# A token-by-weight scaling kernel: six tile sizes replaced by eight equal tiles of 16 tokens

## The chip, the core and the metric

The kernel runs on one core of one Trainium2 chip. Four parts of the core matter here: VectorE (DVE) and ScalarE (ACT), which multiply; SyncE (SP), which computes nothing and issues transfers; and 16 DMA engines, which move data between the chip's main memory (HBM) and the on-chip memory (SBUF, 128 partitions). SP and ACT each own one queue of transfers, and both queues run on the same 16 DMA engines. The metric is the device time of one execution in microseconds (us), as the median of several runs.

## The reference

Every token is a vector of 512 floats, and it is written out twice, each time multiplied by one of its two expert weights. The expert indices are not used.

```python
batch, seq, hidden, k = 16, 1024, 512, 2
def reference(x, expert_indices, expert_weights):
    x_expanded = x[:, :, np.newaxis, :].repeat(k, axis=2)
    return (x_expanded * expert_weights[..., np.newaxis]).astype(np.float32)
```

That is 16,384 tokens: 33.6 MB of x are read, 67.1 MB are written, and the weights are 0.13 MB.

## The kernel before

The 16,384 tokens are 128 for each of the 128 partitions. They are cut into groups of T tokens per partition, and inside a group partition p holds T tokens that follow one another in memory, so that what one partition loads or stores is one contiguous run. I call such a run a row: a load of n tokens has rows of n x 2 KB, a store of n tokens rows of n x 4 KB, and each transfer has 128 rows, 8 for each DMA engine. The groups are five of 24 tokens and one of 8 (`groups`).

Three pools hold the data in SBUF. `w_pool` has all weights in one tile. `x_pool` has two buffers of 24 tokens (TX), `o_pool` two buffers of 12 tokens of output (TO). Together they take 193 KB of each partition.

Three transfers on SP's queue bring the weights at the start. `load(i)` brings input tile i on ACT's queue; the first tile comes in six pieces of 4 tokens, so that computing can begin early, and all others in one transfer. Two loads are issued ahead, and load i + 2 is called after tile i has been computed, since it needs that tile's buffer.

For each token there are two multiplies of a 128x512 slice by one weight per partition. Two of every three go to VectorE, the third to ScalarE (`c % 3 == 2`). When 12 tokens are done, or the tile is at its end, SP stores them. An output buffer can be written again only when the store that reads it, two stores earlier, has landed; an input buffer can be loaded again only when both engines have read all of it.

The framework that builds the kernel adds the semaphore waits, and may move an instruction a few places on its engine's own queue. Each queue is worked in order: a transfer that stands behind a waiting multiply on ACT is not issued before that multiply has started.

Of the kernel before, what the change touches and what calls it, by code (L numbers as in the profile page):

```python
# [1 line left out]

# [4 lines left out]


@with_exitstack
def kernel(  # L10
    ctx: ExitStack,
    tc: tile.TileContext,
    x: bass.AP,
    expert_indices: bass.AP,
    expert_weights: bass.AP,
    out: bass.AP,
):
    nc = tc.nc

    batch, seq, hidden = x.shape  # L20
    k = expert_weights.shape[-1]
    P = nc.NUM_PARTITIONS
    ntok = batch * seq
    assert ntok % P == 0
    A_TOTAL = ntok // P

    f32 = mybir.dt.float32
    row = k * hidden
    TX = 24
    TO = 12  # L30

    groups = [[24], [24], [24], [24], [24], [8]]
    assert sum(sum(g) for g in groups) == A_TOTAL

    xf = x.rearrange("b s h -> (b s) h")
    of = out.rearrange("b s k h -> (b s) (k h)")
    wf = expert_weights.rearrange("b s k -> (b s) k")

    w_pool = ctx.enter_context(tc.tile_pool(name="w_pool", bufs=1))
    x_pool = ctx.enter_context(tc.tile_pool(name="x_pool", bufs=2))  # L40
    o_pool = ctx.enter_context(tc.tile_pool(name="o_pool", bufs=2))

    w_tile = w_pool.tile([P, A_TOTAL * k], f32)

    def rows(of_all, done, T):
        return of_all[done * P : (done + T) * P, :].rearrange(
            "(p a) n -> p (a n)", a=T
        )

    T0 = sum(groups[0])  # L50
    G = len([g for g in groups[1:] if sum(g) == T0])
    head = (1 + G) * T0
    nc.sync.dma_start(out=w_tile[:, : T0 * k], in_=rows(wf, 0, T0))
    nc.sync.dma_start(
        out=w_tile[:, T0 * k : head * k].rearrange("p (g n) -> p g n", g=G),
        in_=wf[T0 * P : head * P, :].rearrange("(g p a) n -> p g (a n)", g=G, p=P),
    )
    nc.sync.dma_start(
        out=w_tile[:, head * k :], in_=rows(wf, head, A_TOTAL - head)
    )  # L60

    tiles = []
    done = 0
    for group in groups:
        T = sum(group)
        a0 = 0
        for n in group:
            tiles.append((done, T, a0, n))
            a0 += n
        done += T  # L70

    loaded = []

    def load(i):
        if i >= len(tiles):
            return
        done, T, a0, n = tiles[i]
        x_tile = x_pool.tile([P, TX * hidden], f32)
        src = rows(xf, done, T)
        step = TX // 6 if i == 0 else n  # L80
        for at in range(0, n, step):
            nc.scalar.dma_start(
                out=x_tile[:, at * hidden : (at + step) * hidden],
                in_=src[:, (a0 + at) * hidden : (a0 + at + step) * hidden],
            )
        loaded.append(x_tile)

    for i in range(2):
        load(i)
    for i, (done, T, a0, n) in enumerate(tiles):  # L90
        x_tile = loaded[i]
        outr = rows(of, done, T)
        for t in range(n):
            if t % TO == 0:
                o_tile = o_pool.tile([P, TO * row], f32)
            for kk in range(k):
                c = (done + a0 + t) * k + kk
                o = t % TO * row + kk * hidden
                if c % 3 == 2:
                    nc.scalar.mul(  # L100
                        out=o_tile[:, o : o + hidden],
                        in_=x_tile[:, t * hidden : (t + 1) * hidden],
                        mul=w_tile[:, c : c + 1],
                    )
                    continue
                nc.vector.tensor_scalar(  # L106
                    out=o_tile[:, o : o + hidden],
                    in0=x_tile[:, t * hidden : (t + 1) * hidden],
                    scalar1=w_tile[:, c : c + 1],
                    scalar2=None,  # L110
                    op0=mybir.AluOpType.mult,
                )
            if (t + 1) % TO == 0 or t + 1 == n:
                at = t // TO * TO
                nc.sync.dma_start(  # L115
                    out=outr[:, (a0 + at) * row : (a0 + t + 1) * row],
                    in_=o_tile[:, : (t + 1 - at) * row],
                )
        load(i + 2)

# [1 line left out]
_INS = ['x', 'expert_indices', 'expert_weights']  # L122
_OUTS = [((16, 1024, 2, 512), 'float32')]


# [23 lines left out]
```

## Time and profile before

| What | Value |
|---|---|
| median of three runs | 240.58 us (239.81 to 240.78) |
| span of the profiled execution, first to last instruction | 238.9 us, 1.7 us less than the median |
| bytes moved | 100.81 MB, mean 422 GB/s |
| VectorE busy | 69.0 us, 171 multiplies |
| ScalarE busy | 54.9 us, 85 multiplies and one table load |
| stores | 10 of 6,144 KB and 1 of 4,096 KB |
| loads | 6 of 1,024 KB, 4 of 6,144 KB, 1 of 2,048 KB |
| weights | 24 KB, 96 KB and 8 KB |

The page of the profile gives busy time per engine, and then the span in 40 slices of 6 us, where a digit is the busy share of a slice in tenths. The share of DMA is the mean over the 16 DMA engines. q1 is SP's queue and q10 is ACT's. A DMA queue's line tells packets, megabytes, and the time its packets took as a share of 16 engines' time; asked for a window, the same line is counted over the packets that start in the window. Besides its rows, each transfer has up to 16 packets of 4 bytes, which signal that an engine has finished. A line of a window of time gives start and end, length, busy time and number of instructions of VectorE, ScalarE and GpSimd, the TensorE clock (of no use here), the DMA share, and GB/s. A packet is counted where it starts, so that short windows can show shares over 1.

### The profile page before, as it was taken

To read this page: it belongs to the slowest core of one execution; us is meant where nothing else is said; L and a number is where in the kernel's file an instruction comes from. 1 tells how busy PE (TensorE), PEld (TensorE's weight loads), DVE (VectorE), ACT (ScalarE), POOL (GpSimd) and SP (SyncE) were. 2 spreads that over 40 slices of the span, in tenths; PEclk is the share of its full clock that TensorE was granted. 3 is DMA by queue.
4 is the path that set the end of the run, shared out by engine and by line. 5 is a ranking of instruction groups with operands and counts; after the bars stand their busy time and mean duration, and the time that the engine had idled before them with its cause. 6 is when DMAs were issued, how large, how long until landed. Compare 5 with 4: busy or idle time off the path is not lost.

```text
span 238.9 us, 364 instructions
## 1 busy us (share of the span) xinstructions
DVE 69.0 (29%) x171; ACT 54.9 (23%) x86; POOL 0.2 (0%) x4
## 2 busy tenths in 40 slices
DVE  0890300004609100190063037003706406415000
ACT  0870300004308000170071034003406106213000
POOL 0000000000000000000000000000000000000000
DMA  6999999999999999999999999999989899999994
GB/s 244 420 443 395 495 395 395 494 428 395 428 494 395 413 494 411 395 446 469 403 411 502 395 420 453 436 411 428 469 379 496 381 428 469 436 411 428 436 439 197
DMA packets 3986, 100.81 MB, mean 422 GB/s; under 512 B 1168, under 2 KB 1168, under 8 KB 1168
## 3 DMA queue, kind: packets, MB, share of 16 engines
q1 hardware_dynamic: 2400, 67.24, 65.2%
q10 hardware_dynamic: 1584, 33.56, 33.1%
q14 instruction: 2, 0.02, 0.0%
HBM read 33.69 MB, written 67.11 MB: 422 GB/s over the span
## 4 chain that ended last, share of the span: by engine, by line
DMA 66%; DVE 13%; another core or an unknown queue 11%; issue 0%; DVEq 0%; SPq 0%
DMA out_dram<-o_tile 54%; DVE o_tile L106 13%; DMA x_tile<-in_x_dram 11%; DVEq L144 0%; DVEq L106 0%; SPq L115 0%
## 5 line engine op out<-in xcount | busy, mean ns | idle before, releaser
L106 DVE TENSOR_SCALAR o_tile<-x_tile,w_tile 128x512 f32<-128x512 f32 x171 | 69.0, 480 | 149.3 <-DMA out_dram<-o_tile 105.3
L100 ACT ACTIVATE o_tile<-x_tile,w_tile 128x512 f32<-128x512 f32 x85 | 53.6, 709 | 155.5 <-DMA out_dram<-o_tile 116.8
L100 ACT ACT_TABLE_LOAD x1 | 1.3, 1283 | 6.7 <-DMA x_tile<-in_x_dram 6.7
L133 POOL MEMSET const-bfloat16-1.0<- 128x1 bf16 x1 | 0.1, 101 | 0.0
L133 POOL MEMSET const-uint8-127<- 128x1 uint8 x1 | 0.1, 101 | 0.0
L133 POOL MEMSET const-float32-0.0<- 128x1 f32 x1 | 0.1, 98 | 0.2 <-issue 0.2
L133 POOL MEMSET const-float32-1.0<- 128x1 f32 x1 | 0.1, 98 | 0.0
## 6 DMA issues: line engine op xcount, KB each, us to landing
out_dram<-o_tile SPq DMA_DIRECT2D x10, 6144.0 KB, 33.6
x_tile<-in_x_dram ACTq DMA_DIRECT2D x4, 6144.0 KB, 43.9
x_tile<-in_x_dram ACTq DMA_DIRECT2D x6, 1024.0 KB, 10.6
out_dram<-o_tile SPq DMA_DIRECT2D x1, 4096.0 KB, 19.5
x_tile<-in_x_dram ACTq DMA_DIRECT2D x1, 2048.0 KB, 24.0
w_tile<-in_expert_weights_dram SPq DMA_DIRECT2D x1, 96.0 KB, 11.1
w_tile<-in_expert_weights_dram SPq DMA_DIRECT2D x1, 24.0 KB, 2.9
w_tile<-in_expert_weights_dram SPq DMA_DIRECT2D x1, 8.0 KB, 13.2
```

The costliest lines, as they stand in the source:

```text
L100: nc.scalar.mul(out=o_tile[:, o : o + hidden], in_=x_tile[:, t * hidden : (t + 1) * hidden], mul=w_tile[:, c : c + 1],)
L106: nc.vector.tensor_scalar(out=o_tile[:, o : o + hidden], in0=x_tile[:, t * hidden : (t + 1) * hidden], scalar1=w_tile[:, c : c + 1], scala ...
L133: nc = _bacc.Bacc("TRN2", target_bir_lowering=False, num_devices=1)
```

## The change

The groups become four of 32 tokens, each in two tiles of 16 (`groups = [[16, 16]] * 4`). Input tiles and output tiles are both 16 tokens: load rows of 32 KB, store rows of 64 KB, two buffers of each. A partition's run in memory is now 64 KB of x and 128 KB of the output for each group, and a tile takes half of it. There are 8 stores instead of 11. The first tile comes in four pieces of 4 tokens and the other seven in one load each, 11 loads as before. The weights come in two transfers on ACT's queue instead of three on SP's: those of the first group behind the first piece of the first tile, all others behind its last piece.

On ACT's queue of the built kernel, the load of the third tile stands behind the first multiply of the second tile; in the kernel before it stood ahead of it.

```diff
-    TX = 24
-    TO = 12
+    TX = 16
+    TO = 16
+    XB = 2
-    groups = [[24], [24], [24], [24], [24], [8]]
+    groups = [[16, 16]] * 4
-    x_pool = ctx.enter_context(tc.tile_pool(name="x_pool", bufs=2))
+    x_pool = ctx.enter_context(tc.tile_pool(name="x_pool", bufs=XB))
     o_pool = ctx.enter_context(tc.tile_pool(name="o_pool", bufs=2))
...
-    nc.sync.dma_start(out=w_tile[:, : T0 * k], in_=rows(wf, 0, T0))
-    nc.sync.dma_start(
-        out=w_tile[:, T0 * k : head * k].rearrange("p (g n) -> p g n", g=G),
-        in_=wf[T0 * P : head * P, :].rearrange("(g p a) n -> p g (a n)", g=G, p=P),
-    )
-    nc.sync.dma_start(
-        out=w_tile[:, head * k :], in_=rows(wf, head, A_TOTAL - head)
-    )
+    def first_weights():
+        nc.scalar.dma_start(out=w_tile[:, : T0 * k], in_=rows(wf, 0, T0))
+
+    def other_weights():
+        nc.scalar.dma_start(
+            out=w_tile[:, T0 * k : head * k].rearrange("p (g n) -> p g n", g=G),
+            in_=wf[T0 * P : head * P, :].rearrange("(g p a) n -> p g (a n)", g=G, p=P),
+        )
...
-        step = TX // 6 if i == 0 else n
+        step = TX // 4 if i == 0 else n
         for at in range(0, n, step):
             nc.scalar.dma_start(
                 out=x_tile[:, at * hidden : (at + step) * hidden],
                 in_=src[:, (a0 + at) * hidden : (a0 + at + step) * hidden],
             )
+            if i == 0 and at == 0:
+                first_weights()
+        if i == 0:
+            other_weights()
...
-    for i in range(2):
+    for i in range(XB):
         load(i)
...
-        load(i + 2)
+        load(i + XB)
```

## The prediction

> **What bounds the kernel now.** I read the page's busy slices first, then its DMA queues, then windows of time, and the chain that ended last only to see the end. Busy slices and queues on the page:
>
> ```profile
> DMA  6999999999999999999999999999989899999994
> q1 hardware_dynamic: 2400, 67.24, 65.2%
> q10 hardware_dynamic: 1584, 33.56, 33.1%
> L106 DVE TENSOR_SCALAR o_tile<-x_tile,w_tile 128x512 f32<-128x512 f32 x171 | 69.0, 480 | 149.3 <-DMA out_dram<-o_tile 105.3
> ```
>
> VectorE works 69 us of 238.9. The 16 DMA engines are busy in every slice but the first and last: 65.2% + 33.1% = 98.3% of the span, 234.8 us per engine. q1 is SP's queue (stores, and in this kernel the weights), q10 is ACT's (loads). The time is therefore what each engine has to move, plus the ends, plus any stretch in which its queues are empty. Windows (length, DVE, ACT, POOL busy, clock, DMA share, GB/s):
>
> ```profile
> 1.00:2.00 1.00, 0.00 (x0) 0.00 (x0) 0.00 (x0) 1.00 0.39 57
> 2.00:3.00 1.00, 0.00 (x0) 0.00 (x0) 0.00 (x0) 1.00 0.64 189
> 140.00:180.00 40.00, 12.85 (x32) 10.02 (x16) 0.00 (x0) 1.00 1.00 434
> 235.00:236.00 1.00, 0.00 (x0) 0.00 (x0) 0.00 (x0) 1.00 0.84 360
> 236.00:237.00 1.00, 0.00 (x0) 0.00 (x0) 0.00 (x0) 1.00 0.08 33
> ```
>
> The middle is full at 434 GB/s. First rows run from about 1.7 us; shares of rows that start fall off after 235, and the last store, issued at 218.4 and landing in 19.5, ends at 237.9.
>
> One row of a transfer (one partition's contiguous run) is one packet, so windows with one size of row price it. Stores alone, 200 to 218 us (48 KB rows) and 228.5 to 234.5 (32 KB):
>
> ```profile
> q1 hardware_dynamic: 176, 7.86, 100.9%
> ...
> q1 hardware_dynamic: 80, 2.62, 101.1%
> ```
>
> 100.9% of 16 engines x 18 us over 160 rows (the other 16 packets only signal) is 1.816 us for 48 KB; 101.1% of 96 us over 80 is 1.213 us for 32 KB. The step is 0.603 us per 16 KB, so a 64 KB row is 2.419 us by extrapolation. From 4 to 13 us (first loads and weights):
>
> ```profile
> q10 hardware_dynamic: 501, 3.64, 96.2%
> q1 hardware_dynamic: 659, 0.11, 6.5%
> ```
>
> 444 rows of 8 KB in 138.5 us: 0.311 us each; small packets 0.014 us each. How two queues share an engine, 140.5 to 159 us (both 48 KB rows) and 176 to 192 us (48 KB stores, 16 KB loads):
>
> ```profile
> q1 hardware_dynamic: 82, 3.98, 49.7%
> q10 hardware_dynamic: 81, 3.93, 49.1%
> ...
> q1 hardware_dynamic: 116, 4.92, 71.3%
> q10 hardware_dynamic: 123, 2.02, 29.4%
> ```
>
> Equal numbers of rows, whatever their size: the engine alternates row by row. The second pair prices 16 KB at 0.612 us (29.4% of 256 us over 123). Last, how late a new transfer starts on a busy engine: load 4 is issued at 127.86, and from 128 to 132.4 only this of it had begun:
>
> ```profile
> q10 hardware_dynamic: 1, 0.05, 2.6%
> ```
>
> So 4.5 to 5 us. Likewise the first store: issued at 13.38, six rows begun by 17.6. Into an idle engine it is 1 us (issue 0.73, rows at 1.7).
>
> VectorE's restarts come from its timeline (start, length, count; in brackets the wait before):
>
> ```profile
> 8.64 2.07 DVE L106 TENSOR_SCALAR o_tile<-x_tile,w_tile 128x512 f32<-128x512 f32 x5 [0.33 <-DMA x_tile<-in_x_dram]
> 11.23 2.07 DVE L106 TENSOR_SCALAR o_tile<-x_tile,w_tile 128x512 f32<-128x512 f32 x5 [0.52 <-DMA x_tile<-in_x_dram]
> 13.79 4.55 DVE L106 TENSOR_SCALAR o_tile<-x_tile,w_tile 128x512 f32<-128x512 f32 x11 [0.49 <-DMA x_tile<-in_x_dram]
> 57.24 6.42 DVE L106 TENSOR_SCALAR o_tile<-x_tile,w_tile 128x512 f32<-128x512 f32 x16 [27.10 <-DMA x_tile<-in_x_dram]
> ```
>
> They go with the pieces of the first load, 2.5 us apart; a multiply takes 0.401 us of such a run.
>
> **The change, part by part.** *Rows.* Each of 11 + 11 transfers of x and out puts 8 rows on each engine. Before: stores 80 x 1.816 + 8 x 1.213, loads 48 x 0.311 + 32 x 1.816 + 8 x 0.612, weights 48 x 0.014: 145.3 + 9.7 + 14.9 + 58.1 + 4.9 + 0.7 = 233.6 us (page: 234.8; the rest is slower first rows and signals). After: stores 64 x 2.419, loads 32 x 0.311 + 56 x 1.213, weights 32 x 0.014: 154.8 + 10.0 + 67.9 + 0.4 = 233.1. Gain 0.5 us. The bytes are the same. Price of the unseen 64 KB row: lower end 2.412 (the line's fixed part, 1.816 - 3 x 0.603 = 0.007 us, gone: 0.4 us more gained over 64 rows); upper end the poorest rate of a full window, 415 GB/s for 8 KB rows against 434, 4.6% of 154.8 = 7 us. I take 2.419, since three sizes lie on one line.
>
> A rule that speaks against the new layout: the Trainium skill, "DMA: Bandwidth & Descriptors", section Latency and other measured facts, has copies between HBM tensors lose rate at row pitches of large powers of two, 207 against 214 GB/s at 512 KiB. The new pitches are 64 KB (loads) and 128 KB (stores) where most were 48 and 96. By it, 3% of 154.8 us would give about 245 us, as an estimate. The smallest pitch there is four times ours, and this trace's last group, whose store pitch is 32 KB, shows 1.213 us a row on the common line; I follow the trace.
>
> *Weights.* SP loses three issues (0.37, 0.42, 0.50 us), ACT gains two of about 0.45 between the pieces of load 0. A 1 MB piece occupies the engines 2.5 us, so later pieces are still issued long before their turn. The weights the first multiply needs come 8 small packets behind piece 1: 0.1 us, inside VectorE's wait for that piece until 5.85. The rest (24 packets, 0.3 us) stands ahead of load 1, needed much later. Price at the start from -1 us (the 0.97 us lost between 1 and 3 us all regained) to +0.4 (one issue bare); I take 0, as the queue of 8 KB rows still has to start up.
>
> *Order at the head.* VectorE resumes on pieces 1 to 4 at 5.85, 8.64, 11.23, 13.79; with fewer small packets between, the fourth comes near 13.4. Then 6 multiplies at 0.401 us (6.42 over 16 in the timeline): store 0 is issued at 15.9 (before: 13.4, after 12 tokens). Until its rows start, about 20, the engines run load 1 from 13.5: 6 of 8 rows. Two remain and alternate with two store rows: load 1 ends at 13.5 + 8 x 1.213 + 2 x 2.419 = 28.0. No gap.
>
> *Loads behind a multiply.* On ACT's queue the third load is now placed behind the first multiply of tile 1, which waits for load 1. It goes out at 29 and starts about 34. Cover: store 0 still has 6 rows, 14.5 us; 3 of them run alone, until 35.2. Then 8 load rows with 7 store rows between: load 2 ends at 61.8, with 2 + 3 + 7 = 12 store rows done, so 4 rows of store 1 are left when tile 2 can start.
>
> *Steady state.* A load row and a store row take 1.213 + 2.419 = 3.63 us, eight pairs 29.1 us, and a tile needs exactly eight of each: the remainder of 4 rows is carried from tile to tile. A tile's 21 multiplies (8.4 us) hide under it; its output buffer is free, since the store two earlier ended long before. VectorE now waits for loads where it waited for stores. That costs nothing: engines stay full.
>
> *The end.* Load 7 ends at 61.8 + 5 x 29.1 = 207.1. Multiplies: landing 0.3, work 8.5, issue and start 1.0 (the idle-engine row): store 7's rows start at 216.9. The cover, 4 rows of store 6, ends at 207.1 + 9.7 = 216.8. So some 0.1 us is bare; before, the last store of 8 tokens was issued at 218.4 while the one ahead, of 205.9, landed 22.4 later: 9.9 us of cover. Each row of cover less costs 2.4 us; each more costs nothing and saves 0.1.
>
> **Sum.** Profiled execution: span 238.9 us; the median of the runs, 240.58, is 1.7 above it, and I carry that over. 238.9 - 0.5 (rows) + 0.1 (end) = 238.5 in the profile; timed, 240.2. I state 240.3.
>
> **Rivals.** *Cover short at the end.* The remainder is 3 rows or fewer when tile 7 starts, so the engines run dry while VectorE multiplies. It decides from one row: if load 2 starts after 35.2 instead of 34, a fourth store row passes alone, and three are left. For it: its lag is read with 48 KB rows, and a row of 64 KB holds an engine longer. Short lags do it too: with the idle engine's 1 us at both places, five pairs run at the head, one store row alone and seven in between, 13 in all. Against it: a short second lag after a long first one leaves six. 3 rows: 240.1 + 2.5 = 242.6; 2 rows: 245.
>
> *Long rows or pitches are slower.* No row speaks for it: 8, 16, 32 and 48 KB lie on one line. At the upper end above, 240.3 + 7 = 247; at a third of that, 242.7.
>
> *64 KB rows are not carried as such*, but as two of 32 KB: 64 more packets, 64 x (2 x 1.213 - 2.419) = 0.4 us, and loads get half the engine instead of a third, so that stores gate and the end is covered: 240.5.
>
> *Faster.* The 0.97 us of the ramp and part of the slowest engine's lag at the end go (234.8 us of work from 1.7 us would end at 236.5, the last landing is at 237.9): -0.5 - 1 gives 239.1. For it: no second queue at the start. Against it: neither lag is tied to weights in any row.
>
> **How the numbers follow.** Forecast 0.49; cover short 0.20; slow rows 0.07; split rows 0.09; faster 0.15. The limit of what can be told from no change is 0.5%, 1.2 us: below 239.4 and above 241.8. Faster 0.17 (rival, and a little of the forecast's spread), slower 0.29 (both slow rivals, and 0.02 of the forecast), same 0.54. The range runs from 239.0, the faster rival, to 242.9, cover short by one row; two rows short and most of slow rows are left out.
>
> **What the profile of the changed kernel would show.** Right: q1 with 1,024 rows of 64 KB and a share near 64.8%; stores-only windows at 2.42 us a row; twice as many bytes from q1 as from q10 in a mixed window, with equal rows; VectorE's wait mostly on x_tile, about 20 us a tile; DMA share 1.00 from 207 to 217. Wrong: a share well below 1 in that stretch (cover short), 2,048 store packets (split), a full-share window clearly under 434 GB/s (slow rows).

## The result, and the profile after

The changed kernel takes 252.14 us (median of four runs, 248.88 to 254.03) against 240.67 for the kernel before on the same chip. The ratio is 1.040, with a 95% interval of 1.037 to 1.043: 4% slower. The forecast was 240.3 and its range ended at 242.9. Medians and ranges are of all executions; the ratios, here and below, leave out those that took over 1.5% more than the fastest of their kernel (here 252.86 and 254.03). Several kernels of this study vary by up to 13 us between executions, and where a profile is of one away from the median, its time is given. The profile of the changed kernel is of an execution of 252.86 us with a span of 251.1.

From its page: busy slices of 6.3 us, DMA queues, and VectorE's largest group.

```profile
DMA  6999989999989999989989999999999998934994
q1 hardware_dynamic: 1152, 67.11, 62.7%
q10 hardware_dynamic: 2128, 33.69, 33.5%
L112 DVE TENSOR_SCALAR o_tile<-x_tile,w_tile 128x512 f32<-128x512 f32 x171 | 68.7, 481 | 160.6 <-DMA x_tile<-in_x_dram 129.2
```

The shares give the first half of the answer. They are 62.7% + 33.5% = 96.2% of 251.1 us, or 241.6 us per engine. Before it was 234.8. So the same bytes cost 6.8 us more of engine time, a mean over 16 engines. The span grew by 12.2 us, so the other 5.4 lie where the engines have nothing to do: 9.5 us now, 4.1 before. The busy slices show where: the digits 3 and 4 in slices 36 and 37, about 220 to 232 us. Windows of the changed kernel (length, DVE, ACT, POOL busy, clock, DMA share, GB/s):

```profile
60.00:100.00 40.00, 12.65 (x32) 11.27 (x19) 0.00 (x0) 1.00 1.01 420
100.00:140.00 40.00, 12.96 (x33) 8.67 (x14) 0.00 (x0) 1.00 0.99 410
140.00:180.00 40.00, 8.40 (x21) 6.85 (x11) 0.00 (x0) 1.00 0.99 407
210.00:220.00 10.00, 0.00 (x0) 0.00 (x0) 0.00 (x0) 1.00 1.00 433
220.00:230.00 10.00, 8.41 (x21) 6.85 (x11) 0.00 (x0) 1.00 0.26 111
```

Two losses, and they are different. From 60 to 180 us the engines are full, yet move 407 to 420 GB/s, where the kernel before moved 433 to 434: rows take longer in the mean. From 220 to 230 us the share is 0.26, so 7.4 us of a mean engine are empty, exactly while VectorE multiplies the last tile.

Rows priced again, first stores alone (231 to 246 us), then the long mixed stretch (20 to 200 us):

```profile
q1 hardware_dynamic: 96, 6.29, 97.0%
```

```profile
q1 hardware_dynamic: 850, 50.20, 65.8%
q10 hardware_dynamic: 860, 25.04, 34.3%
```

Alone, a 64 KB row takes 97.0% of 240 us / 96 = 2.425 us, as forecast (2.419). In the mixed stretch the megabytes make 766 rows of 64 KB and 764 of 32 KB: equal numbers, as forecast. But they take 65.8% of 2,880 us / 766 = 2.474 and 34.3% / 764 = 1.293 us. A pair costs 3.77 us, not 3.63.

These are means, and most rows do not share in the loss. Counted one by one in the trace from 20 to 200 us, 1,245 of the 1,530 rows take what was forecast, 2.42 and 1.21 us within 2%. The other 285 take longer, up to 3.28 and 2.99 us, and cost 6.3 us per engine. In the kernel before, 14 of 1,665 rows are over its prices by so much. So single rows are held up; a row of 64 or 32 KB is not slow as such.

VectorE's timeline shows what gates each tile (start, length, wait before it in brackets):

```profile
34.26 8.40 DVE L112 TENSOR_SCALAR o_tile<-x_tile,w_tile 128x512 f32<-128x512 f32 x21 [17.62 <-DMA x_tile<-in_x_dram]
...
190.37 8.80 DVE L112 TENSOR_SCALAR o_tile<-x_tile,w_tile 128x512 f32<-128x512 f32 x22 [23.24 <-DMA x_tile<-in_x_dram]
220.84 8.41 DVE L112 TENSOR_SCALAR o_tile<-x_tile,w_tile 128x512 f32<-128x512 f32 x21 [21.67 <-DMA x_tile<-in_x_dram]
```

The last tile starts at 220.84, 13.4 us later than the forecast's 207.4. But the trace has 16 completion signals for each transfer, one of each engine (it does not tell which is whose), and these tell a different story than "the load came late". The load of tile 7 completes on the first engine at 201.7, on the median engine at 207.0, and on the last at 220.65. The median engine is on the forecast's time, in part by luck, since at load 2 it was 4.5 us behind it. How far the 16 engines lie apart, as last minus first signal of one load:

```text
load                 1     2     3     4     5     6     7
kernel before     3.9 us at most
changed kernel    5.9   3.4  10.5  11.4  13.9  15.3  18.9 us
```

The queues from 202 to 220 us show the same from another side:

```profile
q1 hardware_dynamic: 116, 7.01, 89.9%
q10 hardware_dynamic: 33, 0.72, 10.0%
```

Stores take 89.9% of the engines' time here: most engines have only stores left, and a few still work on the load that everybody waits for. It lands at 220.65 us. Half of the engines have finished their part of store 6 by 223.9 (the first at 221.0), and the next store is issued only at 229.3.

### The profile page after: what moved, and what is told of

It reads as the page before. It is cut to its first block, busy times and chain, and to the rows that moved or that the text cites. A ratio compares the mean times of both kernels' runs of the same rounds, so it can differ in the third digit from the quotient of the medians.

```text
span 251.1 us, 358 instructions
## 1 busy us (share of the span) xinstructions
DVE 68.7 (27%) x171; ACT 54.6 (22%) x86; POOL 0.2 (0%) x4
## 3 DMA queue, kind: packets, MB, share of 16 engines
q1 hardware_dynamic: 1152, 67.11, 62.7%
q10 hardware_dynamic: 2128, 33.69, 33.5%
## 4 chain that ended last, share of the span: by engine, by line
DMA 50%; DVE 15%; another core or an unknown queue 14%; issue 11%; ACTq 1%; DVEq 0%; SPq 0%; ACT 0%
DMA x_tile<-in_x_dram 33%; DMA out_dram<-o_tile 16%; DVE o_tile L112 15%; ACTq L84 1%; ACTq L59 0%; ACTq L56 0%; DVEq L150 0%; DVEq L112 0%; SPq L121 0%; ACT o_tile L106 0%
```

## The experiments

The expectations name theories by letters. **G**: with load rows half as long as store rows, and row-by-row turns, a load gets one third of an engine and a tile needs exactly one third. VectorE waits for the slowest engine's load. An engine that is ahead empties its stores, then takes its loads alone, and gets further ahead; the spread grows until the end stands bare. **S**: 64 KB rows as such are slow among other traffic. **P**: the row pitches in HBM (64 and 128 KB) are slow. **W**: the place of the weights on ACT's queue does it. **R**, formed only after some of the runs: a load and a store that run in step slow each other. Spread means last minus first completion signal of a load, as above.

**Pitch: one group per tile.** With this edit a tile is contiguous in HBM: pitch 32 KB for loads, 64 KB for stores.

```diff
-    groups = [[16, 16]] * 4
+    groups = [[16]] * 8
```

> Eight groups of 16 tokens instead of four of 32: the rows stay 32 KB and 64 KB, but they follow one another without a gap in memory (pitch 32 KB and 64 KB instead of 64 KB and 128 KB). Theory P (rows of loads and stores disturb each other because the pitches are 64 KB and 128 KB): rows less slow, excess per engine clearly under the 6.5 us of the changed kernel, 243 to 249 us. Theory S (it is the size of the rows, 64 KB stores beside 32 KB loads, whatever the pitch): as the changed kernel, 249 to 254 us.

Measured: 252.04 us (three executions of 252.0 to 255.3, one of 244.44); in the profiled one, of 252.06, the load spread grows to 19.6 us. Its windows:

```profile
100.00:140.00 40.00, 12.22 (x31) 7.94 (x13) 0.00 (x0) 1.00 0.99 411
140.00:180.00 40.00, 8.40 (x21) 6.85 (x11) 0.00 (x0) 1.00 0.99 410
...
220.00:230.00 10.00, 8.30 (x21) 6.58 (x11) 0.00 (x0) 1.00 0.37 157
```

Both losses are as in the changed kernel, at half the pitch.

**Pitch: sizes that are no power of two.** Groups of 48 and 80 tokens, loads with a pitch of 96 and 160 KB, stores 192 and 320 KB (the later weights then come in one contiguous transfer).

```diff
-    groups = [[16, 16]] * 4
+    groups = [[16] * 3, [16] * 5]
```

> Groups of 48 and 80 tokens, in tiles of 16: the rows stay 32 KB and 64 KB, the pitches become 96 and 192 KB, then 160 and 320 KB, none a power of two. Theory P: rows of 1.213 and 2.418 us again, 434 GB/s where loads and stores run together, 240 to 242 us. Theory S: as the changed kernel, 249 to 254 us.

Measured: 251.17 us (three executions of 250.9 to 251.5, one of 244.20); load spreads in that of 251.53: 0.7, 3.8, 4.5, 7.3, 12.7, 19.7, 21.6 us. Windows:

```profile
20.00:60.00 40.00, 8.40 (x21) 6.85 (x11) 0.00 (x0) 1.00 1.03 445
60.00:100.00 40.00, 15.05 (x38) 13.09 (x21) 0.00 (x0) 1.00 1.00 425
100.00:140.00 40.00, 10.55 (x27) 6.85 (x11) 0.00 (x0) 1.00 0.98 407
```

P falls: at every pitch tried, three or four of four executions took 249 to 255 us, and both losses are in the traces. The two executions of 244 do not speak for P, since the next run, at the pitch of the changed kernel, has one of 245 too. The run gives something more. Here the engines start close together, and from 20 to 60 us 64 KB and 32 KB rows run at full pace (445, with 3% of starts borrowed from the next window). The pace is lost only later, while the spread grows. So neither the row sizes nor their mixture must be slow.

**Weights back on SP's queue, at the start.**

```diff
-        nc.scalar.dma_start(out=w_tile[:, : T0 * k], in_=rows(wf, 0, T0))
+        nc.sync.dma_start(out=w_tile[:, : T0 * k], in_=rows(wf, 0, T0))
...
-        nc.scalar.dma_start(
+        nc.sync.dma_start(
...
-            if i == 0 and at == 0:
-                first_weights()
-        if i == 0:
-            other_weights()
...
+    first_weights()
+    other_weights()
     for i in range(XB):
```

> The changed kernel with both weight transfers back on SP's queue at the start. Theories P and S: no effect beyond 0.5 us, 249 to 254 us. Theory W (the weights in the load queue upset the order at the head, and all that follows): 240 to 243 us.

Measured: 247.96 us (245.06 to 251.77), ratio 1.026 (1.020 to 1.033); in the profiled execution, the one of 251.77, the spread still grows to 21.8 us. Most of the loss stays without the moved weights. The ratio is below the 1.040 of the changed kernel and the intervals do not overlap, so up to a third of the loss may go with the weights; with four executions on each side, which differ by 5 to 7 us, it may also be chance.

**Stores in two halves: equal rows.** Each store of 16 tokens becomes two of 8, with 32 KB rows like the loads.

```diff
-                nc.sync.dma_start(
-                    out=outr[:, (a0 + at) * row : (a0 + t + 1) * row],
-                    in_=o_tile[:, : (t + 1 - at) * row],
-                )
+                for h in range(0, TO, 8):
+                    nc.sync.dma_start(
+                        out=outr[:, (a0 + at + h) * row : (a0 + at + h + 8) * row],
+                        in_=o_tile[:, h * row : (h + 8) * row],
+                    )
```

> The changed kernel with each store cut into two of 8 tokens, issued together: store rows of 32 KB, pitches as in the changed kernel, and loads get every second turn of an engine for equal rows. Theory P: rows still slow (5 to 7 us per engine), but the loads run ahead and the end is covered, 245 to 248 us. Theory S: rows at full pace, 240 to 242 us.

Measured: 242.71 us (242.23 to 243.13), ratio 1.009 (1.007 to 1.010). That is 9.4 of the 11.5 us, four fifths of the loss, by an edit that moves the same bytes. It changes one thing besides the row: the first half of a store can go out before the second is computed (10.27 and 15.77 us for store 0, which went out whole at 16.73). The next run has that too. Windows, then VectorE's first two waits (total, times, longest):

```profile
60.00:100.00 40.00, 16.37 (x42) 12.09 (x20) 0.00 (x0) 1.00 1.00 433
...
140.00:180.00 40.00, 8.40 (x21) 6.84 (x11) 0.00 (x0) 1.00 1.01 434
...
220.00:230.00 10.00, 0.00 (x0) 0.00 (x0) 0.00 (x0) 1.00 1.01 436
```

```profile
DVE o_tile L112 <- DMA out_dram<-o_tile: 89.1, 4, 24.2
DVE o_tile L112 <- DMA x_tile<-in_x_dram: 36.0, 4, 17.8
```

The loads now get half of an engine where they need a third, so they are early; VectorE waits mostly for stores, as it did before the change; the spread stays at 3.7 us or less; the pace is back. Both G and S allow this.

**Both halved.** The stores as just shown, and the loads halved too, the later half first. All rows of the later loads are 16 KB, those of the stores 32 KB: the ratio of the changed kernel at half its sizes.

```diff
-        step = TX // 4 if i == 0 else n
-        for at in range(0, n, step):
+        step = TX // 4 if i == 0 else n // 2
+        for at in range(0, n, step) if i == 0 else range(n - step, -1, -step):
```

> The changed kernel with every transfer cut in two: load rows 16 KB (the later half first, so that a tile still starts only when all of it has landed), store rows 32 KB. Rows are half as long, but a load still gets one third of an engine beside a store, so that tiles wait for loads, and for the slowest engine's. Theory G (the order: loads that get only their need gate every tile, engines that are ahead run out of store rows, take loads alone and get further ahead, until some are empty at the end): landings of one load spread to over 8 us between engines by the end, 243 to 252 us. Theory S (rows of 64 KB are the trouble): spread under 4 us, 240 to 242 us.

Measured: 246.22 us (245.89 to 252.35), ratio 1.021 (1.016 to 1.026). The profile is of the execution of 252.35, the others took 245.9 to 246.9. The spread is up to 11.3 us, the pace low again:

```profile
100.00:140.00 40.00, 10.16 (x26) 6.85 (x11) 0.00 (x0) 1.00 1.00 422
140.00:180.00 40.00, 8.40 (x21) 6.85 (x11) 0.00 (x0) 1.00 1.00 422
```

With 32 KB rows as the longest, and the stores of the run above, S would have full pace here; only the ratio of the rows is that of the changed kernel. S falls as the one cause. About half of the loss is here, 2.1 of 4.0%; whether longer rows add the rest is not shown.

**The kernel before, with its loads halved.** The other direction: 24 KB load rows against 48 KB store rows in the kernel that was fine.

```diff
-        step = TX // 6 if i == 0 else n
-        for at in range(0, n, step):
+        step = TX // 6 if i == 0 else n // 2
+        for at in range(0, n, step) if i == 0 else range(n - step, -1, -step):
```

> The kernel before with each load of 24 tokens cut in two (24 KB rows, later half first), its stores unchanged at 48 KB: loads get one third of an engine instead of half. Theory G: the spread between engines grows past 6 us and the kernel slows to 242 to 248 us, less than the changed kernel, since the last tile has 8 tokens. Theory S: 240.5 to 241.5 us.

Measured: 246.89 us (244.12 to 248.09), ratio 1.016 (1.009 to 1.024). In the profiled execution, of 247.95, the spread grows to 15.5 us and at one load 24.4. Windows:

```profile
140.00:180.00 40.00, 12.85 (x32) 10.02 (x16) 0.00 (x0) 1.00 1.00 413
180.00:200.00 20.00, 6.42 (x16) 5.01 (x8) 0.00 (x0) 1.00 1.00 405
```

That is 413 where the kernel before has 434. Same tiles, buffers, stores and weights; loads that get a third of the engine, and both symptoms appear. The head moved as well, though: the eight load transfers hold ACT's queue, ScalarE's table load comes only at 13.5 us, and store 0 goes out at 19.84 instead of 13.38. So the cleaner evidence for G's first half, that the ratio of row sizes starts the drift, is the two runs above, which differ by the load rows alone; this run agrees.

**Other ratios of rows.** In the next kernel a load brings 32 tokens (64 KB rows) and a store takes 8 (32 KB rows), so that loads get two thirds.

```diff
-    TX = 16
-    TO = 16
+    TX = 32
+    TO = 8
...
-    groups = [[16, 16]] * 4
+    groups = [[32]] * 4
...
-        step = TX // 4 if i == 0 else n
+        step = TX // 8 if i == 0 else n
```

> Input tiles of 32 tokens (64 KB load rows) and output tiles of 8 (32 KB store rows), two buffers each, 193 KB as in both kernels, groups and weights as in the changed kernel: a load gets two thirds of an engine, so that tiles wait for stores. Theory G: no growing spread, 240 to 242.5 us. Theory S (64 KB rows beside 32 KB rows): slow rows of 4 us per engine and more, 244 to 252 us.

Measured: 244.17 us (ten runs, 241.97 to 245.76), ratio 1.011 (1.007 to 1.015), load spreads of 2 to 4 us after the first tile (up to 11 within it). It lies between what the theories gave and settles nothing, except that 64 KB load rows can run within about 1% of the kernel before.

Then 32 KB rows on both sides, in three buffers each:

```diff
-    TO = 16
-    XB = 2
+    TO = 8
+    XB = 3
...
-    o_pool = ctx.enter_context(tc.tile_pool(name="o_pool", bufs=2))
+    o_pool = ctx.enter_context(tc.tile_pool(name="o_pool", bufs=3))
```

> Input tiles of 16 tokens in three buffers, output tiles of 8 in three buffers: load and store rows both of 32 KB, 193 KB in all, groups and weights as in the changed kernel. Theory G: a load gets half an engine, three buffers let engines differ by more before one stands empty, no growing spread, 239.5 to 241.5 us. Theory R: depends on the order in which rows meet; 240 to 246 us.

Measured: 248.49 us (244.29 to 251.19), ratio 1.018 (1.010 to 1.026). G's forecast failed. In the profiled execution, the fastest (244.29), the spread is 3 us at most for loads and 5.5 for stores, but load rows are slow in stretches, 1.27 us in the mean instead of 1.213 from 20 to 60 us:

```profile
20.00:60.00 40.00, 11.34 (x29) 9.94 (x16) 0.00 (x0) 1.00 1.00 420
```

An equal share is therefore not enough: there is a second way to lose the pace, without a large spread.

**The end alone.** The last tile of the changed kernel is cut into two of 8 tokens, so that the last store can be issued earlier.

```diff
-    groups = [[16, 16]] * 4
+    groups = [[16, 16]] * 3 + [[16, 8, 8]]
```

> The changed kernel, whose last 16 tokens are cut into two tiles of 8 (load rows 16 KB, store rows 32 KB): after the last load only 4.3 us of multiplies are left instead of 8.5, and half of the last output is queued before. Theory G: about 4 us of the 7 us in which engines stand empty at the end come back, 245 to 250 us, slow rows stay. If the end costs nothing: 249 to 254 us.

Measured: 251.26 us (250.55 to 251.66), ratio 1.041 (1.037 to 1.046): nothing gained. The empty stretch has moved ahead:

```profile
140.00:180.00 40.00, 8.40 (x21) 6.85 (x11) 0.00 (x0) 1.00 0.99 412
180.00:200.00 20.00, 8.80 (x22) 6.24 (x10) 0.00 (x0) 1.00 0.83 354
```

As it looks, once the engines have drifted, whichever tile comes late leaves the early ones without work, and a shorter last tile only changes which: the span has 8.6 us of a mean engine empty, against 9.5.

**The weights of the kernel before, on ACT's queue.** The part of the change that was priced at nothing, done alone: the three weight transfers go behind the first and the last piece of the first load.

```diff
-    nc.sync.dma_start(out=w_tile[:, : T0 * k], in_=rows(wf, 0, T0))
...
+            if i == 0 and at == 0:
+                first_weights()
+        if i == 0:
+            other_weights()
```

> The kernel before with its three weight transfers on ACT's queue, the first behind the first piece of load 0 and the others behind its last piece. Theories G and S: this part of the change moves nothing, 240.2 to 241.2 us. Theory W (weights matter): 242 us and more.

Measured: 250.36 us (250.18 to 251.01), ratio 1.039 (1.035 to 1.043). Only W allowed it (242 us and more), without saying how. Windows, then the queues from 20 to 60 us:

```profile
20.00:60.00 40.00, 6.92 (x18) 5.37 (x9) 0.00 (x0) 1.00 1.02 386
60.00:100.00 40.00, 6.42 (x16) 5.01 (x8) 0.00 (x0) 1.00 0.99 393
...
140.00:180.00 40.00, 11.38 (x29) 10.02 (x16) 0.00 (x0) 1.00 1.00 434
```

```profile
q1 hardware_dynamic: 176, 7.86, 52.2%
q10 hardware_dynamic: 170, 7.57, 49.5%
```

The engines are full and stay together (spreads of 2.3 us or less for the loads and stores that land before 90 us), but 160 store rows take 52.2% of 640 us: 2.09 us each, and 154 load rows 2.06, where 48 KB took 1.816. So rows can be 14% slow in the mean without any drift. What is special here: on ACT's queue the longer head delayed ScalarE's first multiplies (the issue of load 1 held the table load until 8.7 us), store 0 was issued at 15.07 instead of 13.4, and load 1 and store 0 then ran in step. They land at 52.4 and 52.55 us on the last engine, store 1 and load 2 at 85.95 and 85.78. From 100 to 140 us, where they land 3 us apart, the pace is 423, and after that 434.

**Is it the weights, or the step?** Theory R was formed from this: a load and a store that begin and land together, within one row, slow each other; two rows apart they don't. The next runs move load 1 by where it is called. First two kernels with the weights of the run above and load 1 called later:

```diff
-    for i in range(2):
-        load(i)
+    load(0)
...
+            if i == 0 and t == 22:
+                load(1)
```

> The kernel of the run before this (the kernel before with its weights on ACT's queue, 250.4 us), but the second load is issued only after token 22 of the first tile, at about 19 us, so that its rows start about 24 us, some four store rows after store 0's. Theory R (rows are slow while load and store rows of the same place in their transfers, that is of the same partitions, share an engine; in the 250 us run both transfers started and ended together): rows at full pace, 434 GB/s from 20 to 100 us, 240 to 242 us. Theory W (the weights' queue itself costs): 250 us stays.

Measured: 246.92 us (241.41 to 248.24). Load 1 was issued at 28.2 us but its rows did not start before 33.5. Ahead of it in ACT's queue stood the weights' small packets, which landed from 33.5 to 34.2, when store 0 had ended (33.3 to 33.8). Load 1 and store 1 then ran in step, landing at 68.48 and 68.65, and the pace was low again:

```profile
40.00:60.00 20.00, 0.00 (x0) 0.00 (x0) 0.00 (x0) 1.00 1.01 374
```

The run did not do what it was meant for, and it shows the step again.

With `t == 15` in the same place:

> As the run above, but the second load is issued after token 15, about 14 us, while pieces of the first load are still queued ahead of it: its rows start right behind them, near 18 us. Theory R: load 1 and store 0 run closer in step than in the run above; the nearer together they end, the slower: 243 to 250 us if within two rows, 240 to 242 if three or more apart. Theory W: 250 us.

Measured: 248.56 us (247.82 to 249.94), ratio 1.031 (1.026 to 1.036). Load 1 and store 1 land at 66.51 and 66.70 on the last engine; six engines had ended store 1 by 50.2. Windows:

```profile
36.00:62.00 26.00, 0.00 (x0) 0.00 (x0) 0.00 (x0) 1.00 1.00 401
60.00:80.00 20.00, 12.76 (x32) 9.91 (x16) 0.00 (x0) 1.00 0.80 300
100.00:140.00 40.00, 12.85 (x32) 10.03 (x16) 0.00 (x0) 1.00 1.00 433
```

In step, with full engines: 401 GB/s. A fifth of the next 20 us is empty, which is a loss of another kind. Out of step after 100 us: full pace.

Then the weights as in the last kernels (on ACT's queue), all of them behind the first piece, and load 1 called at `t == 8`, so that it starts well away from store 0:

```diff
             if i == 0 and at == 0:
                 first_weights()
-        if i == 0:
-            other_weights()
+                other_weights()
...
+            if i == 0 and t == 8:
+                load(1)
```

> The kernel before with its weights on ACT's queue, all of them behind the first piece of load 0, and the second load issued after token 8, so that ScalarE is not held up and store 0 comes, as in the kernel before, while pieces of load 0 are still queued: load 1 then runs four or more rows behind store 0. Theory R: no slow rows, 240 to 242 us. Theory W: 246 to 251 us.

Measured: ten runs, eight of 240.56 to 241.02 us and two of 250.94 and 253.14; ratio 1.001 (1.000 to 1.002). W falls, as far as it is the queue: weights on ACT's queue, at this place in it, cost nothing in eight executions of ten.

The profiled execution is the one of 250.94, and it speaks against R. One engine trails by 6 to 13 us, and 60 to 100 us moves 411 GB/s, yet on most engines no load and store are in step there. Later, three loads and stores do land together (on the median engine at 123.3 and 123.1 us, 168.9 and 168.8, 203.8 and 203.6). Load 4 and store 5 were issued within 0.02 us of each other, and 15 of their 16 signals came at 168.5 to 169.5 and 168.3 to 169.3. While both ran, from 142 to 168 us:

```profile
142.00:168.00 26.00, 6.43 (x16) 5.01 (x8) 0.00 (x0) 1.00 0.98 423
```

```profile
q10 hardware_dynamic: 113, 5.51, 49.4%
q1 hardware_dynamic: 114, 5.51, 48.9%
```

Over 112 rows each, 49.4% and 48.9% of 416 us are 1.83 and 1.82 us: full pace, in step. (The share is 0.98 since the trailing engine stands apart.) So the step alone does not make rows slow, and R as it stands falls.

The reverse, the kernel before (weights on SP) with load 1 called at `t == 22` (f1 in the expectations), and in a later run at `t == 23`, meant to put load 1 and store 1 in step:

> The kernel before, weights on SP as they were, with one edit: the second load is issued only after token 22 of the first tile. It should start about 33 us together with store 1. Theory R (load and store rows in step are slow): both land together near 66 us instead of 62, slow rows there, 243 to 250 us. Theory W (weights on ACT's queue cost): 240.5 to 241.5 us.

> As f1 (the kernel before, weights on SP), but the second load is issued after token 23, the last of the first tile, some 2 us later, so that its first row comes with the first row of store 1 near 35 us. Theory R (in step is slow): load 1 and store 1 land within 1 us of each other, rows there take 2 us and more on average, and the kernel takes 244 to 250 us. If the step is not the cause: 241 to 242 us, as f1.

Measured: 241.36 us (241.03 to 241.6), ratio 1.003 (1.002 to 1.004), and 241.30 (ten runs, 240.76 to 243.21), ratio 1.004 (1.001 to 1.006). Neither run reached the step: load 1 lands two rows ahead of store 1 (61.3 and 64.9 us in both). The queues of the first from 40 to 60 us:

```profile
q1 hardware_dynamic: 96, 4.72, 54.5%
q10 hardware_dynamic: 80, 3.93, 45.4%
```

54.5% of 320 us over 96 rows and 45.4% over 80 are 1.82 us each: two rows apart there is no slowing at all. The step was never reached with the weights on SP, so these two runs decide nothing about it.

**Is it the same partitions?** In step, a load and a store might be at the same rows of SBUF on the same engine. To change that, the later loads were cut by partitions, 64 to 127 first and then 0 to 63; once in f1 (`t == 22`, weights on SP), once in the changed kernel.

```diff
-            nc.scalar.dma_start(
-                out=x_tile[:, at * hidden : (at + step) * hidden],
-                in_=src[:, (a0 + at) * hidden : (a0 + at + step) * hidden],
-            )
+            for lo, hi in ((0, P),) if i == 0 else ((64, P), (0, 64)):
+                nc.scalar.dma_start(
+                    out=x_tile[lo:hi, at * hidden : (at + step) * hidden],
+                    in_=src[lo:hi, (a0 + at) * hidden : (a0 + at + step) * hidden],
+                )
```

> As f1, but every load from the second on is cut by partitions: 64 to 127 first, then 0 to 63, as two transfers on ACT's queue. Loads and stores run in step as in f1, on other partitions. If rows are slow because both work on the same partitions: 240 to 242 us. If it is only the step: 243 to 250 us, as f1.

> The changed kernel with its loads from the second on cut by partitions, 64 to 127 first. If the slow rows of the changed kernel come from same partitions: rows at full pace and the engines drift less, 240.5 to 245 us. If not: 248 to 254 us.

Measured: 287.89 us (285.55 to 289.98), ratio 1.199 (1.192 to 1.207), and 297.19 (296.42 to 298.09), ratio 1.235 (1.232 to 1.239). The cut brings a cost of its own that buries the question. In the second kernel a half load runs alone from 14 to 19 us; its window and its queue:

```profile
14.00:19.00 5.00, 2.04 (x6) 0.91 (x2) 0.00 (x0) 1.00 1.02 210
```

```profile
q10 hardware_dynamic: 32, 1.05, 102.5%
```

All engines are busy at 210 GB/s: 32 rows in 102.5% of 80 us are 2.56 us each, twice the 1.213 of a 32 KB row. A load into 64 partitions runs at half the rate. The Trainium skill, "SBUF — State Buffer", section Door 1, agrees: a run of 64 partitions reaches only every second one of 16 ports. Its page "DMA: Bandwidth & Descriptors", Rules for kernel authors, says of two partition halves only that they serialize and aren't worth it; here the kernels became 19% and 18% slower than without the cut (287.9 against 241.4 us, 297.2 against 252.1). What the same partitions do remains open.

## Why the prediction was wrong

Point by point, by its steps.

- *Rows.* Right in isolation: the 64 KB row alone takes 2.425 us against 2.419 forecast, and the two queues get equal numbers of rows (766 and 764). The price of a pair in the sum was mis-sized: 3.77 us in the mean instead of 3.63, since 285 of 1,530 rows were held up. With the rest of the bytes that makes 241.6 us per engine where the changed rows were to need 0.5 less than before. That the upper end of the bound (+7 us) is about what happened is luck: it stood for long rows, but the same sizes ran at full pace early in the second pitch run, and 16 and 32 KB rows lost the pace too.
- *Pitch rule of the skill.* Following the trace was right: load and store pitches of 32 and 64, 64 and 128, and 96 to 320 KB gave medians of 251 to 252 us, so no effect shows at these pitches. Its estimate of 245 would have been nearer only by chance.
- *Weights.* Priced at 0: right for the transfer (1.001 in eight of ten runs), and putting them back in the changed kernel left most of the loss, though perhaps not all. What was not seen is that where they stand shifts the head (store 0 at 15.07 instead of 13.38 us), and moving them alone made the kernel before 3.9% slower.
- *Order at the head.* Right to about a microsecond at the median engine: store 0 issued at 16.73 (forecast 15.9), load 1 at 28.7 on the median engine (28.0). But on the last engine it is 34.23, and VectorE starts by the last.
- *Loads behind a multiply.* Right in direction. Load 2 ends at 66.3 on the median engine, 68.2 on the last (forecast 61.8); the forecast missed here that load 1, and so the multiply that stands ahead, waited 6 us for a late engine.
- *Steady state.* This is the step that failed, beside the mis-sized pair of rows: "the remainder of 4 rows is carried from tile to tile", "engines stay full". It treated 16 engines as one. The runs showed in its place that the engines drift apart: the spread of a load's signals went from 3 to 19 us, and each tile started by the latest. From 220 to 230 us 7.4 us of a mean engine stood empty. As G has it, with loads given exactly the share that a tile needs, no engine that is late can catch up, and those ahead run out of stores and load alone; the two runs with halved stores bear this out, but the trace does not tell engines apart, so the drift was not followed engine by engine. In the same passage the forecast noted that VectorE would now wait for loads, and said "That costs nothing". The wait cost nothing as such; what it gave up, by G, was the slack that kept the engines together. On the slowest engine the remainder was 4 rows, if the last signals of load 7 (220.65) and of store 6 (230.3) are of one engine: the arithmetic held for the engine that set the time, and not for the others, which stood empty.
- *The end.* Forecast 0.1 us bare; measured 7.4. The rival "cover short at the end" had the place and the look (a share far below 1 in the last tile's multiplies), but it counted rows of a mean engine and priced 2.4 us a row, and the cause was the spread.
- *Range.* It took one slow cause at a time and left out the larger size of each. Here two came together, 6.8 + 5.4 us. The smaller part is the empty time that the step above should have seen; that the larger part, the held-up rows, comes from the same drift is not shown.

Shown: no pitch tried avoids the loss, and row size alone is not the cause. With the same halved stores, equal load rows bring four fifths of the loss back, and load rows of half that size bring drift and held-up rows again. The changed kernel loses its 12.2 us to 6.8 us of held-up rows and 5.4 us of empty engines. Open: why single rows are held up. Drift is not needed for it (the kernel before with its weights on ACT's queue: 386 GB/s, spreads of 2.3 us), an equal share does not always prevent it (three buffers: 1.018), and being in step does not decide it (386 and 374 GB/s in two runs, 1.83 us a row in another). One rival was not tested: a conflict in HBM between the addresses that the engines read and write at the same moment. The pitch runs changed the distance between rows, but not this. No version tried beats the kernel before; the nearest, with late load 1 and the weights on ACT's queue, equals it in most runs.

## What to carry to other kernels

Where two queues share DMA engines that take turns row by row, the ratio of row sizes is the ratio of bandwidth: a stream that gates the next tile and gets just what it needs is a risk to look for. Giving it clearly more took 252.1 to 242.7 us here, but two other layouts with half or two thirds for the loads stayed at 248.5 and 244.2, so it has to be measured. A sum over a mean engine says what the bytes cost, not when a tile can start: look at the completion signals of the slowest engine, and at whether their spread grows from tile to tile. And cut transfers along the free dimension, not by halves of the partitions.

## What the runs showed of the hardware

- Rows of a load and a store in step took 2.06 to 2.09 us for 48 KB in one run and 1.82 to 1.83 in another; two rows apart they took 1.82.
- Rows are not slowed evenly. In the changed kernel 285 of 1,530 took over 2% more than alone, up to 2.5 times as long; in the kernel before, 14 of 1,665.
- With the weights moved, and store 0 issued 1.7 us later, a kernel went from 240.7 to 250.4 us.
- Small packets are held back by long rows of another queue. In the run with `t == 22` and the weights on ACT's queue, 143 of the later weights' 640 packets started from 20 to 33 us, beside the 48 KB rows of store 0; the other 497, 0.011 to 0.015 us each, all started from 33.0 to 33.8 us, as the store ended (33.3 to 33.8). The load behind them, issued at 28.2, began no earlier.
- The same kernel can end 10 us and more apart in two executions without any change in it (244.4 to 255.3 us in the first pitch run; 240.6 to 241.0 or 251 to 253 with late load 1); why was not shown, since each has one trace. The medians of the kernel before beside the other runs were 240.6 to 241.1.
- Loads into 64 partitions: 210 GB/s with all engines busy, 2.56 us for a 32 KB row that takes 1.21 in a load into 128.
